# Expert blocks and row gathers on one core: gathers of the U phase bound behind U blocks, columns dealt anew, transposes moved, a score tile widened

## The chip, the cores and the metric

One core of a Trainium2 chip runs the whole program. The metric is the time of one execution on the device in microseconds (us); what counts is the median of several runs. Each run is timed without a profile, and one more execution is profiled. A difference of 0.2% is about what the measurement can tell from no change.

The engines run side by side and wait for each other by semaphores: PE (matrix products), DVE (vector work), ACT (activations and copies), POOL (here: a few vector operations, and the issue of gathers), SP (the issue of plain transfers). Sixteen DMA engines move the data of all queues.

## The reference

One layer of a hybrid decoder: a combined input projection, a convolution branch, a state-space branch, an output projection, and then an expert mixer over 16384 experts. The change touches the mixer alone:

```python
def peer_block(xb, w_q, keys, U, V):
    T = xb.shape[0]
    q = (xb @ w_q).reshape(T, PEER_HEADS, 2, D_KEY // 2)          # 8 heads, 2 halves of 128
    s = jnp.einsum('thcd,hckd->thck', q, keys).astype(jnp.float32) # 128 keys each
    s1, i1 = lax.top_k(s[:, :, 0], PEER_TOPK)                      # 16 of 128
    s2, i2 = lax.top_k(s[:, :, 1], PEER_TOPK)
    cand = (s1[..., :, None] + s2[..., None, :]).reshape(T, PEER_HEADS, PEER_TOPK * PEER_TOPK)
    sc, f = lax.top_k(cand, PEER_TOPK)
    ids = (jnp.take_along_axis(i1, f // PEER_TOPK, axis=-1) * N_KEYS
           + jnp.take_along_axis(i2, f % PEER_TOPK, axis=-1))
    g = jax.nn.softmax(sc, axis=-1)
    act = jax.nn.gelu(jnp.einsum('thkd,td->thk', U[ids], xb).astype(jnp.float32), approximate=False)
    w = (g * act).astype(xb.dtype)
    return jnp.einsum('thk,thkd->td', w, V[ids])
```

Each of the 320 tokens that are left at this point chooses 128 experts (8 heads, 16 each), and its output is the sum of their V rows, weighted by gate times gelu of the U row's product with the token.

## The kernel before, in words

The mixer takes two ways at once. 128 tokens (and 8 more) are **gathered**: for each of their picks, a column of 128 expert numbers is fetched by an indirect transfer that brings 128 rows of 2048 numbers (a U row and a V row side by side, 8 KB) into one of five buffers `wuv`. There are 136 such columns. The other 184 tokens are **dense**: the kernel computes them against all experts, in 128 blocks of U (each 128 experts by 1024, 512 KB) and then 128 blocks of V, and a matrix of gates zeroes what a token did not choose.

The order of the program:

- *Queries and scores* (`for j in range(16)`): 16 blocks of `w_q` give `qT`, and three products with `keys` give the scores of the three token tiles of `KTILES`: 128 gathered tokens, 128 and 64 others. The third product has 64 columns of `qT` as its stationary side. DVE finds the top 16 of the gathered tile at once (`heads`); the other two are left to background tasks (`topk_tasks(1)`, `topk_tasks(2)`).
- *U phase.* `u_block(b)` loads block b into a ring of eight buffers (`eraw`, from SP's queue), and PE makes 8 products, each of which the profile records as two: 16 records to a block. The last product's name goes into `ustep`. Behind each block a `Feed` hands out background tasks, so that all are dealt evenly: up to block 84 (`SB`) the top-k tasks of the dense tokens mixed with `NU[0]` picks; from block 84 on the first half of the gate steps (`g_step`, PE `pg`, DVE `oh`) with `NU[1]` picks.
- *V phase.* `v_block(b)` the same, with the product's name in `vstep`; beside its first 64 blocks the second half of the gate steps and `NU[2]` picks, then the rest of the picks up to block 126.

A *pick* of column n (`pick_row`) is DVE's dot product of the U half with the token (`pick_dot`), two tiny ACT operations, and DVE's weighted sum of the V half of the column before (`pick_sum`), which frees a buffer. Before a dot product, `ahead` issues the gathers of the next columns (four, later two). `gather` issues one on POOL's queue, and ties it to the block that lies `LEAD` = 4 blocks behind the last one issued: it starts only when PE has finished that block. In the kernel before, the list that this counts from leaves out U's first 84 blocks, so that the gathers beside them are tied to no block.

When a dense tile's top 16 are known, `place` transposes the picks and gates on PE into `pix`; `PLACE` names the U blocks behind which the transposes of the two tiles stand in PE's order. PE works in the order of its queue: if such a transpose waits for DVE, all blocks behind it wait.

A scheduler sorts the instructions of each engine by a simulated time, within what these bounds and the data allow.

Of the kernel before, what the change touches and what calls it, by code (L numbers as in the profile page):

```python
# [7 lines left out]
F32 = mybir.dt.float32  # L8
# [15 lines left out]
T = TP + NQ * TS  # L24
# [11 lines left out]
T2 = 320  # L36
# [16 lines left out]
SB = 84  # L53
HB = 64
KTILES = ((0, NGAT), (128, 128), (256, 64))
NU = (42, 28, 37)
LM = (0.05, 0.05, 0.1, 0.5, 0.999)
LOW = 400
NW0 = 3
# [3 lines left out]
DEEP = 4  # L63
NEAR = 2
GLAG = 14
PLACE = (38, 50)
LASTP = 126
XW = 70
XR = 86
# [75 lines left out]
def body(tc, ia, oa, stop=None):  # L145
    nc = tc.nc
    with ExitStack() as top:
# [58 lines left out]
        def pj(name="pj"):  # L206
            return ps.tile([128, PJ], F32, name=name, tag="pj", bufs=3)[:, :T]

        def pj2(name="pj"):
            return pj(name)[:, :T2]  # L210
# [32 lines left out]
        def proj(out, w, act, first=True, last=True):  # L243
            for k in range(KD):
                for c_ in range(2):
                    mm(out, w[0][:, k, :], act(k)[c_], start=(first and k == 0 and c_ == 0), stop=False)
            for k in range(KD):
                mm(out, w[1][:, k, :], act(k)[0], start=False, stop=(last and k == KD - 1))

        def weight(src, i):  # L250
            raw = wp.tile([128, KD, 128], F32, name="wraw", bufs=rb[0])
            nc.sync.dma_start(raw, src[i].rearrange("p (k m) -> p k m", m=128))
            h = wp.tile([128, KD, 128], F32R, name="wh", bufs=2)
            l = wp.tile([128, KD, 128], F32R, name="wl", bufs=2)
            nw[0] += 1
            f_ = lm[0]
            on_dve = int((nw[0] + 1) * f_) > int(nw[0] * f_)
            split(h, l, raw, on_pool=not on_dve, on_dve=lm[0] == 1)
            return h, l
# [3 lines left out]
        def rows(h, l):  # L263
            return lambda k: (h[:, k, :], l[:, k, :])

        def misc(shape, name):
            return ps.tile(shape, F32, name=name, tag="misc", bufs=2)
# [64 lines left out]
        p = misc([128, T], "pn1")  # L332
# [11 lines left out]
        t = tp.tile([128, T], F32, name="rst", tag="yo", bufs=2)  # L344
# [177 lines left out]
        def xbc(g):  # L522
            tiles = [pair(F32, "xg"), None]

            def step(c_, j):
                if c_ == 2:
                    tiles[1] = pair(F32, "bc")
                pf = project(8 * g + c_)
                p = pf[:, :T]
                cat = tp.tile([128, MCAT], F32, name="mcat", bufs=2)  # L530
                cpr, csm = cat_fill(cat, MC, mcache[:, j, :])
                nc.scalar.activation(cpr[:, NM:], p[:, :SQ], AF.Identity, bias=V("b_in", 8 * g + c_))
                nc.scalar.activation(cpr[:, :NM], p[:, T2:], AF.Identity, bias=V("b_in", 8 * g + c_))
                nc.scalar.activation(csm, samp(p[:, SQ:T2]), AF.Identity, bias=V("b_in", 8 * g + c_))
                cat_save(cat, MC, mnew[:, j, :])
                conv_short(cat, j, tiles[c_ // 2][:, c_ % 2, :], pf[:, :MCAT])

            return tiles, [lambda c_=c_, j=j: step(c_, j) for c_, j in enumerate((2 * g, 2 * g + 1, 16 + g, 24 + g))]
# [311 lines left out]
        for g in range(G):  # L850
            new = ssd(g, *tiles, sz)
            if g + 1 < G:
                tiles, steps = xbc(g + 1)
# [48 lines left out]
        for j in range(KD):  # L902
# [4 lines left out]
            p = pj2()  # L907
# [7 lines left out]
        for j in range(KD):  # L915
            w = weight(ia["w_o"], j)
            p = pj2()
# [13 lines left out]
        p = ps.tile([128, T], F32, name="pn2", tag="pb", bufs=1)  # L931
# [30 lines left out]
        qp = qs.enter_context(tc.tile_pool(name="qp", bufs=1))  # L962
# [7 lines left out]
        for c_ in range(2):  # L970
            p = misc([128, 512], "px")
# [4 lines left out]
        p = misc([128, 4], "prs")  # L976
# [7 lines left out]
        def extra_tokens():  # L984
            E0 = NGAT + ND
            nc.gpsimd.memset(acce, 0.0)
            xe = qp.tile([128, 128], F32, name="xe", bufs=2)
            nc.gpsimd.tensor_copy(xe.rearrange("p (q t) -> p q t", t=NX),
                                  rs2[:, None, E0:T2].to_broadcast([128, XQ, NX]))
            p = misc([128, 4], "prs")  # L990
            nc.tensor.matmul(p[:, 3:4], xe, ident[:, 0:1], start=True, stop=True)
            nc.scalar.copy(rsT[:, 3:4], p[:, 3:4])
            for c_ in range(2):
                p = misc([128, 512], "px")
                cs = slice(c_ * 512, c_ * 512 + 512)
                for k in range(4):
                    xe = qp.tile([128, 128], F32, name="xe", bufs=2)
                    nc.gpsimd.tensor_copy(xe.rearrange("p (q t) -> p q t", t=NX),
                                          xT[:, 4 * c_ + k, None, E0:T2].to_broadcast([128, XQ, NX]))
                    nc.tensor.transpose(p[:, k * 128:(k + 1) * 128], xe, ident)  # L1000
                nc.scalar.copy(acce[:NX, cs], p[:NX])
                nc.vector.scalar_tensor_tensor(x2e[:, cs], p, rsT[:, 3:4], n2r[:, cs], op0=OP.mult, op1=OP.mult)

        keys = qp.tile([128, 16, NK], F32, name="keys")
        nc.sync.dma_start(keys, ia["keys"])

        def top16(vals, idx, v, h, late=False):
            L = v.shape[0]
            i_ = nc.vector.max(vals[:L, h, 0:8], v)
            if late:  # L1010
                tc.add_manual_dep(i_.ins, early[0], mybir.DependencyInfo(mybir.DependencyClass.NoSync,
                                                                         mybir.DependencyReason.DATA),
                                  reason="gathered tokens first")
            nc.vector.max_index(idx[:L, h, 0:8], vals[:L, h, 0:8], v)
            nc.vector.match_replace(v, vals[:L, h, 0:8], v, -3.0e38)
            nc.vector.max(vals[:L, h, 8:16], v)
            nc.vector.max_index(idx[:L, h, 8:16], vals[:L, h, 8:16], v)
# [73 lines left out]
        ustep, vstep = [], []  # L1091

        def gather(c):
            u = gp.tile([128, 2 * D], F32, name="wuv", bufs=UV)
            i_ = nc.gpsimd.indirect_dma_start(out=u, out_offset=None, in_=ia["peer_uv"],  # L1095
                                              in_offset=bass.IndirectOffsetOnAxis(ap=gid[:, c:c + 1], axis=0))
            steps = ustep[SB:] + vstep
            if len(steps) > LEAD:
                tc.add_manual_dep(i_.ins, steps[-1 - LEAD], mybir.DependencyInfo(mybir.DependencyClass.Sync,
                                                                          mybir.DependencyReason.DATA),  # L1100
                                  reason="rows after blocks")
            return u

        def ahead(n):
            for i_ in range(n, min(n + (DEEP if len(vstep) <= HB else NEAR), NCOL)):
                if i_ not in pend:
                    pend[i_] = gather(COLS[i_])

        for j in range(16):
            w = weight(ia["w_q"], j)  # L1110
            p = pj()
            proj(p[:, :T2], w, rows(ah[:, :, :T2], al[:, :, :T2]))
            qT = qp.tile([128, T], F32, name="qT", bufs=3)
            nc.scalar.copy(qT[:, :T2], p[:, :T2])
            p = misc([128, 3, NK], "psc")
            for i, (t0, L) in enumerate(KTILES):
                nc.tensor.matmul(p[:L, i], qT[:, t0:t0 + L], keys[:, j, :], start=True, stop=True)
                s_ = sall[:, i - 1, j] if i else kp.tile([128, NK], F32, name="sco", bufs=9)
                nc.scalar.copy(s_[:L], p[:L, i])
                if i == 0:  # L1120
                    top16(sv[i], si[i], s_[:L], j)
            if j == EXTRA:
                extra_tokens()
            if j % (2 * HG) == 2 * HG - 1:
                heads(j // 2 - HG + 1)
            if j == 2 * HG - 1:
                ahead(0)
# [10 lines left out]
        def topk_tasks(i):  # L1138
# [34 lines left out]
            def place():  # L1173
                n_ = min(L, NGAT + ND - t0)
                p = misc([128, 3, 128], "pix")
                for c_, v in enumerate((st[0], st[1], st["g"])):
                    i_ = nc.tensor.transpose(p[:, c_, :L], v[:L], ident[:L, :L])
                    tc.add_manual_dep(i_.ins, ustep[PLACE[i - 1]], mybir.DependencyInfo(mybir.DependencyClass.NoSync,
                                                                              mybir.DependencyReason.DATA),
# [68 lines left out]
        t1, t2 = topk_tasks(1), topk_tasks(2)  # L1248
        bg = mixin(t1[:-1] + t2[:-5] + t1[-1:] + t2[-5:-1], take(NU[0] - 4)) + take(4) + t2[-1:]

# [81 lines left out]
        Sm.append(s1p.tile([128, 128 - SB, ND], F32, name="S1"))  # L1332
        feed = Feed(mixin(g_tasks(0), take(NU[1])), 128 - SB - 2)
        for b in range(SB, 128):
# [65 lines left out]

        feed = Feed(mixin(g_tasks(1), take(NU[2])), HB - 2)
        for b in range(HB):
# [109 lines left out]
```

## Time and profile before

| | |
|---|---|
| median of 3 runs | 1330.94 us |
| lowest, highest | 1330.91, 1332.9 us |
| the profiled execution | 1334.54 us |
| its span, first to last instruction | 1332.8 us |
| PE, DVE, ACT, POOL busy | 1294.1, 993.7, 524.5, 583.1 us |
| moved by the DMA engines | 373.68 MB, of it 142.62 MB by the gathers |

Times in the profile count from the start of the span. A row of a timeline has the start, the duration, the engine, the line and operation, tiles written and read, and in square brackets how long the engine was idle ahead of it and what ended that. A row of busy time by stretches has the stretch, and for each engine its busy time and the number of instructions; then the granted share of PE's clock, the busy share of the DMA engines, and what they moved in GB/s. A group's row has the count, the busy time, the mean in ns, and the idle time of its engine ahead of it. q0 is the queue of the gathers, q1 SP's.

### The profile page before, as it was taken

To read this page: it belongs to the slowest core of one execution; us is meant where nothing else is said; L and a number is where in the kernel's file an instruction comes from. 1 tells how busy PE (TensorE), PEld (TensorE's weight loads), DVE (VectorE), ACT (ScalarE), POOL (GpSimd) and SP (SyncE) were. 2 spreads that over 40 slices of the span, in tenths; PEclk is the share of its full clock that TensorE was granted. 3 is DMA by queue.
4 is the path that set the end of the run, shared out by engine and by line. 5 is a ranking of instruction groups with operands and counts; after the bars stand their busy time and mean duration, and the time that the engine had idled before them with its cause. 6 is when DMAs were issued, how large, how long until landed. Compare 5 with 4: busy or idle time off the path is not lost.

```text
span 1332.8 us, 23897 instructions
## 1 busy us (share of the span) xinstructions
PE 1294.1 (97%) x9004; PEld 1225.6 (92%) x9004; DVE 993.7 (75%) x2324; ACT 524.5 (39%) x1377; POOL 583.1 (44%) x484
## 2 busy tenths in 40 slices
PE   9999999999999999999999898999999999999997
PEld 7888888888888999988999898999999999999997
DVE  7888778877877335799999987458977888644453
ACT  6777777777765444433322221121210111101012
POOL 2477767876684666744222252032332323122210
PEclk9999999999999999999999999999999999999999
DMA  6434453454434344637999999799999999999992
GB/s 242 161 127 170 166 172 129 153 180 150 157 99 159 129 156 143 210 114 277 381 414 415 377 397 414 282 416 413 396 413 414 415 414 416 398 395 415 414 413 107
DMA packets 85892, 373.68 MB, mean 280 GB/s; under 512 B 9984, under 2 KB 15488, under 8 KB 66192
## 3 DMA queue, kind: packets, MB, share of 16 engines
q1 hardware_dynamic: 65024, 227.52, 46.5%
q0 software_dynamic: 19584, 142.62, 26.2%
q10 hardware_dynamic: 1168, 2.02, 0.4%
q8 instruction: 71, 1.16, 0.3%
q14 instruction: 45, 0.37, 0.1%
HBM read 359.05 MB, written 13.06 MB: 279 GB/s over the span
## 4 chain that ended last, share of the span: by engine, by line
PE 73%; DVE 17%; DMA 7%; ACT 2%; issue 1%; POOL 0%; DVEq 0%; ACTq 0%; POOLq 0%
PE pj L159 29%; PE va L1378 21%; PE pj L1284 12%; DMA eraw<-in_uT_dram 3%; DMA eraw<-in_vE_dram 3%; DVE ygat L1215 2%; DVE wuv L1207 2%; PE pst L159 2%; PE pg L1312 1%; PE po L159 1%; PE py L159 1%; DVE pcv L482 1%; PE pdec L159 1%; DVE cand L1060 1%; PE ptr L164 1%
## 5 line engine op out<-in xcount | busy, mean ns | idle before, releaser
L1095 POOL DMA_INDIRECT wuv<-in_peer_uv_dram,gid x136 | 184.2, 1354 | 490.9 <-PE va L1378 151.6
L1284 PE MATMUL pj<-nd,eraw 128*128 128x184 f32 x2048 | 332.6, 323 | 8.7 <-DMA eraw<-in_uT_dram 5.2
L1284 PEld LDWEIGHTS pj<-nd,eraw 128*128 128x128 f32 x2048 | 321.9, 191 | 11.3 <-ACT S L1286 6.9
L227 POOL TENSOR_TENSOR wl<-wraw,wh 128x1024 fp32r<-128x1024 f32 x111 | 267.2, 2408 | 148.2 <-ACT wh L226 77.3
L1378 PE MATMUL va<-S,eraw 128*128 128x184 f32 x2048 | 326.7, 320 | 2.7 <-DMA eraw<-in_vE_dram 2.6
L1378 PEld LDWEIGHTS va<-S,eraw 128*128 128x128 f32 x2048 | 318.8, 190 | 5.9 <-DMA eraw<-in_vE_dram 4.1
L159 PE MATMUL pj<-ah,wh 128*128 128x336 f32 (+1 forms) x768 | 242.5, 327 | 0.7 <-ACT xnf L202 0.7
L159 PE MATMUL pj<-al,wh 128*128 128x336 f32 (+1 forms) x768 | 233.0, 317 | 0.0
L1215 DVE SCALAR_TENSOR_TENSOR ygat<-wuv,scg,ygat 128x1024 f32<-128x1024 f32 x128 | 164.0, 1281 | 52.2 <-ACT scg L1210 50.5
L1207 DVE SCALAR_TENSOR_TENSOR wuv<-wuv,x2m 128x1024 f32<-128x1024 f32 x128 | 156.0, 1219 | 62.8 <-DMA wuv<-in_peer_uv_dram,gid 62.8
L1209 ACT ACTIVATE scg<-scg 128x1 f32<-128x1 f32 x136 | 27.5, 202 | 403.7 <-DVE wuv L1207 403.4
L226 ACT CAST wh<-wraw 128x1024 fp32r<-128x1024 f32 x125 | 131.2, 1050 | 115.2 <-PE pj L159 70.1
L482 DVE SCALAR_TENSOR_TENSOR pcv<-ccat,vec,pcv 128x256 f32<-128x256 f32 x464 | 148.7, 379 | 17.1 <-ACT pcv L480 17.1
L159 PEld LDWEIGHTS pj<-ah,wh 128*128 128x128 f32 x768 | 146.3, 191 | 8.7 <-ACT xnf L202 2.8
L159 PEld LDWEIGHTS pj<-al,wh 128*128 128x128 f32 x768 | 145.8, 191 | 0.7
L159 PE MATMUL pj<-ah,wl 128*128 128x336 f32 (+1 forms) x768 | 136.8, 315 | 1.3 <-DVE wl L227 1.3
L159 PEld LDWEIGHTS pj<-ah,wl 128*128 128x128 f32 x768 | 119.5, 188 | 2.7 <-DVE wl L227 1.6
L1286 ACT ACTIVATE S<-pj 128x184 f32<-128x184 f32 x128 | 38.7, 319 | 140.2 <-PE pj L1284 140.1
L496 DVE SCALAR_TENSOR_TENSOR pj<-mcat,vec,pj 128x360 f32<-128x360 f32 x96 | 56.3, 587 | 3.7 <-ACT pj L494 3.7
L1319 DVE SCALAR_TENSOR_TENSOR S<-pg,S 128x352 f32<-128x352 f32 (+1 forms) x69 | 33.2, 508 | 32.7 <-PE pg L1312 30.4
L202 ACT ACT_TABLE_LOAD x39 | 50.0, 1283 | 0.7
L1210 ACT ACTIVATE scg<-scg,ggw 128x1 f32<-128x1 f32 x136 | 40.0, 294 | 4.3
(365 smaller groups left out, 1645.1 us busy)
## 6 DMA issues: line engine op xcount, KB each, us to landing
eraw<-in_uT_dram SPq DMA_DIRECT2D x128, 512.0 KB
eraw<-in_vE_dram SPq DMA_DIRECT2D x128, 512.0 KB
wraw<-in_w_in_dram SPq DMA_DIRECT2D x80, 512.0 KB
st<-in_state_dram SPq DMA_DIRECT2D x8, 1024.0 KB
out_ssm_s_dram<-st SPq DMA_DIRECT2D x8, 1024.0 KB
wraw<-in_w_mo_dram SPq DMA_DIRECT2D x16, 512.0 KB
wraw<-in_w_q_dram SPq DMA_DIRECT2D x16, 512.0 KB
wraw<-in_w_co_dram SPq DMA_DIRECT2D x8, 512.0 KB
```

The costliest lines, as they stand in the source:

```text
L159: i_ = nc.tensor.matmul(*a_, **kw)
L202: i_ = nc.scalar.activation(out, in_, f, **kw)
L226: (nc.vector.tensor_copy if on_dve else nc.scalar.copy)(h, src)
L227: (nc.gpsimd if on_pool else nc.vector).tensor_tensor(l, src, h.bitcast(F32), op=OP.subtract)
L482: t = nc.vector.scalar_tensor_tensor(o, i_, wv, a_, op0=OP.mult, op1=OP.add)
L496: nc.vector.scalar_tensor_tensor(o, cat[:, w:w + n], wv, o, op0=OP.mult, op1=OP.add)
L1095: i_ = nc.gpsimd.indirect_dma_start(out=u, out_offset=None, in_=ia["peer_uv"], in_offset=bass.IndirectOffsetOnAxis(ap=gid[:, c:c + 1], axi ...
L1207: nc.vector.scalar_tensor_tensor(u[:, :D], u[:, :D], 1.0, x2m if c < NPICK else x2e, op0=OP.mult, op1=OP.mult, accum_out=w)
L1210: nc.scalar.activation(w, w, AF.Copy, scale=ggw[:, c:c + 1])
L1215: nc.vector.scalar_tensor_tensor(a_, u[:, D:], scg[:, c:c + 1], a_, op0=OP.mult, op1=OP.add)
L1284: i_ = nc.tensor.matmul(p[:, :ND], raw[:, k, :], nd[:, k, :], start=(k == 0), stop=(k == KD - 1))
L1378: i_ = nc.tensor.matmul(va[k // 2][:, k % 2], raw[:, k, :], Sv(b), start=False, stop=(b == 127), skip_group_check=True)
```

## The change

Four numbers or places change. The list from which `gather` counts takes in all U blocks. Columns are dealt 46, 26, 36 and 28 to the four stretches instead of 42, 28, 37 and 29. The transposes stand behind U blocks 42 and 55 instead of 38 and 50. The third score product takes 128 columns of `qT`, of which the last 64 are zeros (three fixed tiles of 384 columns, whose ends POOL sets to zero once), and gives 128 rows, of which 64 are used as before.

```diff
-NU = (42, 28, 37)
+NU = (46, 26, 36)
-PLACE = (38, 50)
+PLACE = (42, 55)
 ...
-            steps = ustep[SB:] + vstep
+            steps = ustep + vstep
             if len(steps) > LEAD:
 ...
+        qTs = [qp.tile([128, 384], F32, name=f"qT{i}") for i in range(3)]
+        for t in qTs:
+            nc.gpsimd.memset(t[:, T2:], 0.0)
 ...
-            qT = qp.tile([128, T], F32, name="qT", bufs=3)
+            qT = qTs[j % 3]
 ...
-                nc.tensor.matmul(p[:L, i], qT[:, t0:t0 + L], keys[:, j, :], start=True, stop=True)
+                nc.tensor.matmul(p[:, i], qT[:, t0:t0 + 128], keys[:, j, :], start=True, stop=True)
```

POOL's queue, before: the gathers number 45 to 49 (from 0). `DMASW` is the semaphore of an earlier gather on the same lane, `DVE_49` the release of the buffer, `PE_49` a block.

```order
L1095 DMA wuv<-in_peer_uv_dram,gid 128x2048 [waits DMASW0_49,DVE_49]
L1095 DMA wuv<-in_peer_uv_dram,gid 128x2048 [waits DMASW1_49,DVE_49]
L1095 DMA wuv<-in_peer_uv_dram,gid 128x2048 [waits DMASW2_49,DVE_49,PE_49]
L1095 DMA wuv<-in_peer_uv_dram,gid 128x2048 [waits DMASW3_49,DVE_49,PE_49]
L1095 DMA wuv<-in_peer_uv_dram,gid 128x2048 [waits DMASW4_49,DVE_49,PE_49]
```

And the same lanes now:

```order
L1095 DMA wuv<-in_peer_uv_dram,gid 128x2048 [waits DMASW0_49,DVE_49,PE_49]
L1095 DMA wuv<-in_peer_uv_dram,gid 128x2048 [waits DMASW1_49,DVE_49,PE_49]
L1095 DMA wuv<-in_peer_uv_dram,gid 128x2048 [waits DMASW2_49,DVE_49,PE_49]
L1095 DMA wuv<-in_peer_uv_dram,gid 128x2048 [waits DMASW3_49,DVE_49,PE_49]
L1095 DMA wuv<-in_peer_uv_dram,gid 128x2048 [waits DMASW4_49,DVE_49,PE_49]
```

Numbers 45 and 46 waited for no block and now wait for one; by the semaphores' values, numbers 42 to 50 wait for U blocks 68, 71, 72, 73, 74, 75, 77, 80 and 82, where 47 to 50 waited for 84, 85, 87 and 88.

PE's queue, before: the U blocks around the transposes. A count of 8 is one block.

```order
L1284 MATMUL pj<-nd,eraw 128x184 x264
L1177 MATMUL pix<-cst,pick_8164 128x128
L1177 MATMUL pix<-cst,pick_8225 128x128
L1177 MATMUL pix<-cst,gsm 128x128
L1284 MATMUL pj<-nd,eraw 128x184 x96
L1177 MATMUL pix<-cst,pick_8939 128x64
L1177 MATMUL pix<-cst,pick_8970 128x64
L1177 MATMUL pix<-cst,gsm 128x64
L1284 MATMUL pj<-nd,eraw 128x184 x120
```

And now:

```order
L1287 MATMUL pj<-nd,eraw 128x184 x296
L1180 MATMUL pix<-cst,pick_8178 128x128
L1180 MATMUL pix<-cst,pick_8227 128x128
L1180 MATMUL pix<-cst,gsm 128x128
L1287 MATMUL pj<-nd,eraw 128x184 x104
L1180 MATMUL pix<-cst,pick_8935 128x64
L1180 MATMUL pix<-cst,pick_8984 128x64
L1180 MATMUL pix<-cst,gsm 128x64
L1287 MATMUL pj<-nd,eraw 128x184 x80
```

The first three transposes stand four blocks later and the second three five. On DVE 24 picks stand ahead of the first tile's results instead of 23, and 32 ahead of the second's instead of 29.

PE's queue in the score stage, one piece of the difference: products with `keys` (`psc`) between those of the queries (`pj`).

```order
-L1117 MATMUL psc<-keys,qT 128x128
-L1117 MATMUL psc<-keys,qT 64x128
+L1120 MATMUL psc<-keys,qT_6662 128x128
+L1120 MATMUL psc<-keys,qT_6661 128x128
 L159 MATMUL pj<-ah,wl 128x320 x6
-L1117 MATMUL psc<-keys,qT 64x128
-L1117 MATMUL psc<-keys,qT 128x128
+L1120 MATMUL psc<-keys,qT_6662 128x128
+L1120 MATMUL psc<-keys,qT_6663 128x128
```

All score products are now of one form. Their places are the same but for single swaps.

## Prediction

> **What bounds the kernel now.** I read the page first, then busy time by stretches, then the queues in one stretch, then POOL's timeline and PE's waits.
>
> ```profile
> span 1332.8 us, 23897 instructions
> PE   9999999999999999999999898999999999999997
> DMA  6434453454434344637999999799999999999992
> GB/s 242 161 127 170 166 172 129 153 180 150 157 99 159 129 156 143 210 114 277 381 414 415 377 397 414 282 416 413 396 413 414 415 414 416 398 395 415 414 413 107
> q0 software_dynamic: 19584, 142.62, 26.2%
> eraw<-in_uT_dram SPq DMA_DIRECT2D x128, 512.0 KB
> ```
>
> Each digit is one fortieth of the span, 33.3 us. From the nineteenth on the DMA stands near 415 GB/s, with one clear hole: 282 in slice 26. This is where expert blocks (0.524 MB each, 128 U and 128 V) and the 136 gathers (142.62 MB / 136 = 1.049 MB each) share the engines. The next table cuts that part up; its last two columns are DMA share and GB/s.
>
> ```profile
> core 0: us, PE busy (x) PEld busy (x) DVE busy (x) ACT busy (x) POOL busy (x), PEclk, DMA share, GB/s
> 616.00:640.00 24.00, 21.75 (x123) 19.54 (x121) 23.37 (x109) 7.51 (x25) 9.82 (x10) 0.93 0.98 389
> 640.00:720.00 80.00, 79.08 (x504) 78.17 (x505) 79.69 (x295) 22.00 (x72) 19.88 (x16) 1.00 1.00 400
> 720.00:780.00 60.00, 52.93 (x325) 51.67 (x324) 57.80 (x149) 13.50 (x49) 17.22 (x12) 0.97 0.98 383
> 780.00:803.00 23.00, 23.00 (x150) 23.00 (x149) 17.53 (x24) 6.76 (x27) 12.88 (x8) 1.00 1.02 417
> 803.00:829.00 26.00, 21.51 (x181) 20.28 (x181) 18.79 (x31) 4.25 (x16) 5.24 (x6) 1.00 1.02 414
> 829.00:861.00 32.00, 31.99 (x242) 31.51 (x241) 19.82 (x33) 5.83 (x22) 0.80 (x1) 1.00 0.82 305
> 861.00:870.00 9.00, 9.00 (x60) 9.00 (x59) 0.86 (x2) 1.19 (x4) 2.82 (x3) 1.00 0.84 312
> 870.00:982.00 112.00, 109.83 (x899) 108.13 (x898) 90.08 (x150) 23.09 (x86) 36.72 (x24) 1.00 1.01 409
> 982.00:1144.00 162.00, 160.13 (x1286) 155.83 (x1285) 135.21 (x235) 18.43 (x72) 46.83 (x35) 1.00 1.02 415
> 1144.00:1162.00 18.00, 17.17 (x121) 16.55 (x120) 12.26 (x17) 2.48 (x10) 1.19 (x1) 1.00 1.01 403
> 1162.00:1320.00 158.00, 158.00 (x1016) 158.00 (x1015) 71.97 (x93) 17.10 (x61) 33.08 (x27) 1.00 0.93 372
> ```
>
> The last row is V from block 64 on: 1016 records, 16 to a block, in 158 us: PE without a pause at 2.49 us a block. No transfer can shorten it; a gain must come before 1162. There the DMA is the limit, so I keep a ledger of bytes: what each stretch is short of 415 GB/s, turned into time. 616 to 640: (415-389)*24/415 = 1.5 us; then 2.9, 4.6, 0, 0, **8.5**, 2.2, 1.6, 0, 0.5: 21.8 us in all, half of it between 829 and 870.
>
> ```profile
> 824.42 1.21 POOL L1095 DMA_INDIRECT wuv<-in_peer_uv_dram,gid  x1 [6.64 <-DVE ygat L1215]
> 828.12 1.68 POOL L1095 DMA_INDIRECT wuv<-in_peer_uv_dram,gid  x1 [2.48 <-DVE ygat L1215]
> 861.13 0.94 POOL L1095 DMA_INDIRECT wuv<-in_peer_uv_dram,gid  x1 [31.33 <-PE pj L1284]
> 863.62 0.94 POOL L1095 DMA_INDIRECT wuv<-in_peer_uv_dram,gid  x1 [1.55 <-PE pj L1284]
> 803.00:829.00 26.00, 19.91 (x117) 17.89 (x117) 1.00 1.02 414
> 829.00:861.00 32.00, 31.18 (x194) 29.92 (x193) 1.00 0.82 305
> ```
>
> The hole is a pause of the gathers. Up to number 46 (from 0) they are bound to no block; number 47 is the first that is, to U block 84, and POOL waits 31.33 us for it. The last two rows count U-block records alone: while gathers ran free before the pause, 117 records made 7.3 blocks in 26 us, 3.6 us a block instead of 2.49; in the pause 12.1 blocks came in 32 us and the ring of eight block buffers filled.
>
> ```profile
> DMA packets 1514, 8.30 MB, mean 415 GB/s; under 512 B 162, under 2 KB 162, under 8 KB 840
> q0 software_dynamic: 755, 5.51, 66.6%
> q1 hardware_dynamic: 758, 2.78, 34.7%
> ```
>
> These rows (800 to 820) show why blocks starve: both queues move equally many packets, but a gather's are twice as large, so gathers (q0) take two thirds.
>
> **The change, part by part.** *Binding and columns.* Gathers 47 to 50 no longer wait for blocks 84, 85, 87, 88 but for 75, 77, 80, 82, since four more columns are dealt behind U's first 84 blocks; 42 to 46, free before, wait for 68 to 74. The fifth gather and those before stay free; numbers 5 to 41 get bounds that are no later than the blocks beside which they ran, so these rarely bite. POOL's queue holds only gathers here, so behind a waiting one stands just the next; the one who waits is DVE's dot product. In the pause the DMA had (415-305)*32 us = 3.5 MB free, and 0.9 MB to 870; the four gathers are 4.2 MB. They fit: **-10.7 us** (8.5 + 2.2). Bounds: 0, if the pause turns up elsewhere, and -10.7. I take the full value, because the four bounds lie evenly across the pause and DVE has 12 us free in it (19.82 of 32) for four picks:
>
> ```profile
> L1215 DVE SCALAR_TENSOR_TENSOR ygat<-wuv,scg,ygat 128x1024 f32<-128x1024 f32 x128 | 164.0, 1281 | 52.2 <-ACT scg L1210 50.5
> L1207 DVE SCALAR_TENSOR_TENSOR wuv<-wuv,x2m 128x1024 f32<-128x1024 f32 x128 | 156.0, 1219 | 62.8 <-DMA wuv<-in_peer_uv_dram,gid 62.8
> L1312 PE MATMUL pg<-oh 128*128 128x64 f16 x736 | 30.6, 193 | 0.3 <-DVE oh L1308 0.2
> ```
>
> A pick is 1.22 + 1.28 = 2.5 us, four are 10. Ahead of V block 64 there are now 111 gathers, not 110: 1.049 MB at 415 GB/s is **+2.5 us**; behind it one fewer, which is worth nothing beside PE's 158 us. After U block 84, 60 gathers instead of 63 stand beside 108 blocks: 119.5 MB, 288 us; PE needs 108*2.49 and, for the 38 of 46 steps of the gate matrices that stand behind it, 38/46 of 30.6: 294. So PE is next, and what is late after the hole is gone is PE itself, by little.
>
> A figure of the Trainium skill speaks against this value: DMA: Bandwidth & Descriptors, Specifications, gives about 358 GB/s as the limit of one core's share of HBM. By it the pause would hold only (358-305)*32/358 = 4.7 us, and the sum below would be 3.8 us smaller; the rows sustain 415, so the measurement decides.
>
> *Transposes.* PE waited for DVE ahead of them:
>
> ```profile
> PE pix L1177 <- DVE pick L1061: 5.3, 2, 2.8
> ```
>
> The first set stands four blocks (10.0 us) later, with one more pick (2.5 us) ahead of it on DVE: its wait goes. The second stands five blocks (12.4 us) later with three more picks (7.5 us), but PE comes 2.8 us earlier for the first wait and some 2 us for the next part: 2.8 + 7.5 + 4.8 - 12.4 = 2.7 us of wait stay. The ledger has 4.6 us short from 720 to 780, when PE stalled with a full ring: between -4.6 and +2.7 (the wait comes back and nothing else does) I take half of the gain, **-2.3 us**, one of two waits.
>
> *Third score tile.* Narrow tiles cost PE more than their columns:
>
> ```profile
> 573.47 0.60 PE L1117 MATMUL psc<-keys,qT 128*128 128x128 f32 x4
> 573.83 1.13 PE L159 MATMUL pj<-ah,wl 128*128 128x320 f32 x6
> 591.72 0.75 PE L1117 MATMUL psc<-keys,qT 128*128 128x128 f32 x4
> 592.39 1.16 PE L159 MATMUL pj<-ah,wl 128*128 128x320 f32 x6
> 594.33 0.37 PE pj L159 x3
> 594.73 0.28 DVE sv L1009
> 615.72 8.11 DMA wuv<-in_peer_uv_dram,gid
> ```
>
> Four full-width records hold PE for 0.36 us until the next line starts; the four at 591.72, of which two are the 64-wide ones, for 0.67. So 0.31 us a tile, 16 tiles, at most -5.0. The last three rows are of the chain: PE carries it to 594.7, then DVE to the first gather at 615.72. Seven narrow tiles stand before 594.7: **-2.2 us**; the other nine run beside DVE or the ring. Zero is the other bound. The three memsets cost POOL less than 0.95 us each (a fourfold larger one below) and stand ahead of a wait of 4.09 us: nothing.
>
> ```profile
> 550.72 5.00 POOL L227 TENSOR_TENSOR wl<-wraw,wh 128x1024 fp32r<-128x1024 f32 x2 [4.09 <-PE pj L159]
> 556.67 0.95 POOL L986 MEMSET acce<- 128x1024 f32 x1 [0.94 <-DVE vec L223]
> ```
>
> Sum: -10.7 + 2.5 - 2.3 - 2.2 = **-12.7 us**. The profiled execution took 1334.54 us (span 1332.8), the median is 1330.94; that 0.3% doesn't matter to a difference of microseconds. Forecast: 1318.2 us.
>
> **The rivals.** (1) *Blocks starve in place of the pause.* For it: the equal packet counts. A gather at 5.51 MB / 20 us takes 3.8 us, in which 0.53 MB of blocks land, one block, while PE could use 1.5. If the ring is empty by then, each of the four gathers costs PE 1.3 us: 5.1 us back, 1323.3. Against it: free bytes are free bytes, and gathers 42 to 46 come later. The Trainium skill has it as a rule (DMA: Bandwidth & Descriptors, Queues, rings and completion order: an engine takes turns between queues, packet by packet); by that rule the time is this one, and 755 against 758 packets agree with it. (2) *The pause only moves.* 42 to 46 are held for two to four blocks and the DMA idles at 804 to 829 instead. Then only +2.5 and -2.2 stay: 1331.2. Against it: PE starves there, so blocks take every byte until eight buffers are full. (3) *Everything fills.* All 21.8 us go: 1330.9 - 21.8 + 2.5 - 2.2 = 1309.4. Against it: the shortfalls at 616 to 720 have other causes (a late ACT, DVE at 79.69 of 80). (4) *Slower: the second transposes.* DVE is full until 780, and with both queues full the gather at 824.42 came after 6.64 us of waiting and 1.2 us of the one before, 7.9 us, where a pick takes 2.5. If five picks ahead of the transposes stretch so, DVE is 27 us late, PE stops with a full ring, the gathers bound to its blocks stop too: 1318.2 + 27 = 1345. It decides from some 13 us of lateness on. Against it: DVE was busy for 79.69 of 80 us and 57.80 of 60 up to 780, so landings hardly held it.
>
> **How the numbers follow.** Forecast 0.58, (1) 0.15, (2) 0.10, (3) 0.10, (4) 0.07. This measurement tells 0.2% (2.7 us) from no change: (2) is "same", (4) slower, the rest faster: 0.83, 0.10, 0.07. The range runs from (3) to the point where the hole is half filled and nothing else comes (1330.9 - 5.3 + 2.5 = 1328): 1309 to 1328, which leaves out (2) and (4), 0.17.
>
> **What would show it.** Right: no gap of POOL over 10 us between 800 and 900, that slice of the GB/s row near 415, U block 84 some 8 to 12 us earlier, no wait at the first transposes, score records of one form with 0.11 us between them. V from block 64 still 158 us. Wrong: a new pause of gathers, a wait of PE for the second transposes far over 3 us, or blocks at 3.6 us where the pause was.

## Result, and the profile after

| | before | after |
|---|---|---|
| median, runs beside each other | 1331.3 us (1330.91 to 1332.9, 4 runs) | 1321.76 us (1320.57 to 1323.37, 4 runs) |
| ratio, 95% interval | | 0.9927 [0.991, 0.9944] |
| the profiled execution, its span | 1334.54, 1332.8 us | 1323.37, 1321.6 us |

The change saves 9.5 us by the medians and 11.2 by the two profiled executions. The forecast of 1318.2 was 3.6 us too low; the result lies between it and the first rival's 1323.3, nearer to the rival, and inside the range.

Three lines of the page of after, then its busy time by stretches with the columns of the prediction's table (lines L1284, L1378, L1177, L1312, L1117 of before are L1287, L1381, L1180, L1315, L1120 now):

```profile
span 1321.6 us, 23911 instructions
PE   9999999999999999998999998999999999999997
GB/s 244 162 128 172 161 178 111 174 168 163 156 90 158 130 158 144 200 128 272 354 408 415 378 417 415 414 413 414 415 413 416 414 411 415 387 398 409 413 407 86
```

```profile
616.00:640.00 24.00, 18.66 (x113) 16.39 (x111) 22.46 (x102) 8.63 (x30) 8.69 (x9) 1.00 1.00 406
640.00:720.00 80.00, 79.43 (x499) 79.36 (x499) 79.66 (x289) 21.84 (x72) 19.31 (x15) 0.98 0.99 388
720.00:780.00 60.00, 57.70 (x368) 56.57 (x367) 56.74 (x144) 14.28 (x53) 20.04 (x13) 1.00 1.00 396
780.00:803.00 23.00, 22.58 (x170) 22.32 (x169) 19.50 (x30) 5.33 (x22) 9.07 (x6) 1.00 1.02 414
803.00:829.00 26.00, 22.87 (x170) 21.90 (x169) 18.03 (x32) 4.63 (x18) 5.75 (x5) 1.00 1.02 415
829.00:861.00 32.00, 30.93 (x253) 30.18 (x252) 23.69 (x39) 6.00 (x23) 7.30 (x6) 1.00 1.02 413
861.00:870.00 9.00, 9.00 (x74) 8.83 (x73) 7.52 (x13) 1.47 (x5) 1.88 (x2) 1.00 1.03 416
1151.00:1309.00 158.00, 158.00 (x1016) 158.00 (x1015) 69.33 (x91) 16.61 (x59) 31.05 (x26) 1.00 0.92 365
```

Slice 26 of the GB/s line went from 282 to 414, and 829 to 861 from 305 to 413: the hole is gone. V from block 64 on is the same 1016 records in the same 158 us. Two things are not as good as they look: from 803 to 829 PE is still busy for only 22.87 of 26 us (21.51 before), and 640 to 720 is now short of 415 GB/s by 27*80/415 = 5.2 us, where it was 2.9.

POOL's timeline, all gathers of after that start between 805 and 853, shows how the hole was filled:

```profile
805.67 1.00 POOL L1095 DMA_INDIRECT wuv<-in_peer_uv_dram,gid  x1 [4.75 <-PE pj L1287]
817.01 0.94 POOL L1095 DMA_INDIRECT wuv<-in_peer_uv_dram,gid  x1 [10.33 <-PE pg L1315]
820.21 1.02 POOL L1095 DMA_INDIRECT wuv<-in_peer_uv_dram,gid  x1 [2.26 <-DVE oh L1311]
823.11 0.94 POOL L1095 DMA_INDIRECT wuv<-in_peer_uv_dram,gid  x1 [1.89 <-PE pg L1315]
826.61 1.86 POOL L1095 DMA_INDIRECT wuv<-in_peer_uv_dram,gid  x1 [2.56 <-DVE oh L1311]
830.92 0.94 POOL L1095 DMA_INDIRECT wuv<-in_peer_uv_dram,gid  x1 [2.45 <-PE pj L1287]
839.04 1.19 POOL L1095 DMA_INDIRECT wuv<-in_peer_uv_dram,gid  x1 [7.19 <-DVE ygat L1218]
848.35 1.86 POOL L1095 DMA_INDIRECT wuv<-in_peer_uv_dram,gid  x1 [8.12 <-DVE oh L1311]
852.04 1.19 POOL L1095 DMA_INDIRECT wuv<-in_peer_uv_dram,gid  x1 [1.83 <-DVE ygat L1218]
```

The longest gap is 10.33 us instead of 31.33.

The table below holds all kernels of this study, from their profiled executions. U0, U84 and V64 stand for the first product of that block. MB is what all queues moved from U0 to V64, "short" is that time less the MB at 415 GB/s. The runs' names are explained with the experiments.

| kernel | U0 to U84, us | U84 to V64 | V64 to end | MB | short, us | gathers landed by U84, by V64 |
|---|---|---|---|---|---|---|
| before | 242.9 | 303.2 | 171.4 | 217.34 | 22.4 | 47, 110 |
| b_bind | 232.7 | 302.9 | 171.0 | 217.23 | 12.2 | 46, 110 |
| b_deal | 245.5 | 297.0 | 170.9 | 218.68 | 15.6 | 51, 111 |
| b_place | 240.4 | 301.5 | 170.9 | 217.39 | 18.1 | 47, 110 |
| b_wide | 243.1 | 301.3 | 171.2 | 217.53 | 20.3 | 47, 110 |
| after | 239.1 | 299.2 | 171.0 | 218.79 | 11.1 | 49, 111 |
| a_olddeal | 232.2 | 301.9 | 171.1 | 217.08 | 11.1 | 46, 110 |
| a_free | 242.8 | 299.1 | 171.3 | 218.80 | 14.7 | 51, 111 |
| a_narrow | 237.6 | 300.9 | 171.2 | 218.80 | 11.3 | 49, 111 |
| a_oldplace | 239.5 | 299.7 | 170.9 | 218.75 | 12.1 | 49, 111 |
| c_few_u | 230.4 | 297.6 | 174.3 | 214.56 | 11.0 | 46, 107 |
| c_few_v | 238.3 | 298.4 | 174.3 | 214.69 | 19.4 | 49, 107 |
| d_40 | 227.5 | 299.5 | 175.6 | 214.01 | 11.2 | 44, 107 |
| d_38 | 227.9 | 299.2 | 181.4 | 211.82 | 16.6 | 42, 106 |

Before U0 the change shows in one place: from the first score product to U0 all with narrow tiles take 57.5 us and all with wide ones 54.7 or 54.8. Ahead of that product, where the kernels hardly differ, the traces scatter: it starts between 556.3 and 559.1 us.

A single profiled execution is not exact to a microsecond. That of before is 3.2 us over its median, that of b_place 2.75 under its own (1328.35 and 1331.1).

### The profile page after: what moved, and what is told of

The parts are those of the page before. It is cut to its first block, busy times and chain, and to the rows that moved or that the text cites. A ratio compares the mean times of both kernels' runs of the same rounds, so it can differ in the third digit from the quotient of the medians.

```text
span 1321.6 us, 23911 instructions
## 1 busy us (share of the span) xinstructions
PE 1288.1 (97%) x9004; PEld 1224.5 (93%) x9004; DVE 990.6 (75%) x2324; ACT 522.5 (40%) x1377; POOL 578.9 (44%) x487
## 4 chain that ended last, share of the span: by engine, by line
PE 74%; DVE 16%; DMA 7%; ACT 2%; issue 1%; ACTq 0%; DVEq 0%; SPq 0%
PE pj L159 30%; PE va L1381 22%; PE pj L1287 13%; DMA eraw<-in_uT_dram 3%; DMA eraw<-in_vE_dram 3%; PE pst L159 2%; DVE wuv L1210 2%; DVE ygat L1218 2%; PE pg L1315 1%; PE po L159 1%; PE py L159 1%; DVE pcv L482 1%; PE pdec L159 1%; DMA wuv<-in_peer_uv_dram,gid 1%; DVE si L1017 1%
## 5 line engine op out<-in xcount | busy, mean ns | idle before, releaser
L1095 POOL DMA_INDIRECT wuv<-in_peer_uv_dram,gid x136 | 179.8, 1322 | 487.0 <-PE va L1381 126.1
L1287 PE MATMUL pj<-nd,eraw 128*128 128x184 f32 x2048 | 333.4, 322 | 7.5 <-DMA eraw<-in_uT_dram 3.9
L1287 PEld LDWEIGHTS pj<-nd,eraw 128*128 128x128 f32 x2048 | 320.3, 191 | 9.8 <-ACT S L1289 7.4
L1381 PE MATMUL va<-S,eraw 128*128 128x184 f32 x2048 | 326.1, 320 | 1.8 <-DMA eraw<-in_vE_dram 1.6
L1381 PEld LDWEIGHTS va<-S,eraw 128*128 128x128 f32 x2048 | 318.9, 190 | 3.5 <-DMA eraw<-in_vE_dram 2.2
```

Of the source, the lines that this page charges most:

```text
L1287: i_ = nc.tensor.matmul(p[:, :ND], raw[:, k, :], nd[:, k, :], start=(k == 0), stop=(k == KD - 1))
L1381: i_ = nc.tensor.matmul(va[k // 2][:, k % 2], raw[:, k, :], Sv(b), start=False, stop=(b == 127), skip_group_check=True)
```

## Experiments

**Each part alone in the kernel before.** Four kernels, timed on one chip beside before (1331.81 us).

b_bind, the binding alone:

```diff
-            steps = ustep[SB:] + vstep
+            steps = ustep + vstep
```

> The kernel before with the binding alone: gathers beside U's first 84 blocks are tied to blocks, columns dealt 42, 28, 37 as before. Gathers 36 to 46 now wait for U blocks 62 to 82, number 47 for 84 as before. Theory (bytes: the pause was transfer time thrown away, and the starved blocks ahead of it are its other side): the pause of 31 us is spread out, blocks at 803 to 829 no longer take 3.6 us, U block 84 begins some 8 us earlier, the time is 1323, 8 us less than before (5 to 10). Rival (the pause only moves, since the same 47 gathers stand ahead of block 84): within 2 us of 1331.

Measured: 1324.39 us (1323.92 to 1325.12), ratio 0.9945 [0.9933, 0.9958]: 7.4 us less, close to the theory's 8. Three stretches of its busy time:

```profile
803.00:829.00 26.00, 26.00 (x216) 25.65 (x215) 19.87 (x34) 4.46 (x17) 5.37 (x5) 1.00 1.01 399
829.00:861.00 32.00, 32.00 (x259) 31.65 (x257) 24.84 (x42) 6.31 (x24) 8.10 (x6) 1.00 1.02 413
861.00:870.00 9.00, 9.00 (x80) 8.88 (x79) 7.70 (x13) 1.96 (x8) 1.50 (x2) 1.00 1.02 416
```

Four gathers of POOL's timeline:

```profile
801.93 0.94 POOL L1095 DMA_INDIRECT wuv<-in_peer_uv_dram,gid  x1 [4.46 <-PE pg L1312]
815.82 1.16 POOL L1095 DMA_INDIRECT wuv<-in_peer_uv_dram,gid  x1 [12.96 <-DVE ygat L1215]
818.32 0.94 POOL L1095 DMA_INDIRECT wuv<-in_peer_uv_dram,gid  x1 [1.34 <-PE pj L1284]
821.38 1.16 POOL L1095 DMA_INDIRECT wuv<-in_peer_uv_dram,gid  x1 [2.12 <-PE pj L1284]
```

The queues from 800 to 820 (packets, MB, share of the engines):

```profile
q1 hardware_dynamic: 1704, 5.21, 68.1%
q0 software_dynamic: 356, 2.65, 32.5%
```

The hole is filled here without any gather more ahead of block 84. Number 47 is still bound to block 84; it is the earlier ones that are held back. From the packets of q0, 1.049 MB to a gather, number 41 (from 0) lands at 829.8 instead of 814.4, number 46 at 854.9 instead of 837.6, and 47 at 859.8 instead of 868.4. In the place of the held gathers the blocks come: q1 moves 5.21 MB from 800 to 820 instead of 2.78, PE is busy in all of the 26 us from 803 to 829, and U block 72 starts at 815.4 instead of 825.6.

b_deal, the dealing alone (`NU` 42, 28, 37 to 46, 26, 36):

> The kernel before with the columns dealt 46, 26, 36 alone, gathers beside U's first 84 blocks still tied to no block. Four more gathers run freely ahead of block 84, number 51 is the first that waits. Theory: the pause shrinks from 31 us to some 18, blocks starve at 3.6 us for some 15 us longer, block 84 is no earlier, but 60 instead of 63 gathers stand between it and V block 64: the time is 1326, 5 us less than before (2 to 7). Rival (the dealing does it all, the binding only rarely bites): 1322 or less, as with the whole change.

Measured: 1330.64 us (1328.8 to 1333.58), ratio 0.9988 [0.998, 0.9997]: 1.2 us less, and both expectations missed. Two stretches of its busy time:

```profile
829.00:861.00 32.00, 28.61 (x229) 27.47 (x228) 19.64 (x33) 5.60 (x21) 5.03 (x4) 1.00 1.02 410
861.00:870.00 9.00, 9.00 (x72) 8.94 (x71) 9.00 (x17) 1.97 (x7) 2.59 (x2) 1.00 0.80 274
```

PE's waits for blocks between 803 and 870 (us in total, times, longest), in before:

```profile
PE pj L1284 <- DMA eraw<-in_uT_dram: 4.1, 5, 1.1
```

In b_deal:

```profile
PE pj L1284 <- DMA eraw<-in_uT_dram: 6.2, 8, 1.1
```

And in after; b_bind has no such wait there:

```profile
PE pj L1287 <- DMA eraw<-in_uT_dram: 3.9, 5, 1.1
```

The four gathers fill the hole, 410 GB/s, but they take the bytes of the blocks: PE is busy for 28.61 of 32 us and waits 6.2 us for blocks. U0 to U84 takes 245.5 us, 2.6 more than before, though the DMA moves at full rate. A new short hole follows (274). What comes back is behind U84, where three gathers fewer stand.

b_place, the transposes alone (`PLACE` 38, 50 to 42, 55), and b_wide, the wide tile alone:

```diff
-            qT = qp.tile([128, T], F32, name="qT", bufs=3)
+            qT = qTs[j % 3]
 ...
-                nc.tensor.matmul(p[:L, i], qT[:, t0:t0 + L], keys[:, j, :], start=True, stop=True)
+                nc.tensor.matmul(p[:, i], qT[:, t0:t0 + 128], keys[:, j, :], start=True, stop=True)
```

> The kernel before with the transposes of picks behind U blocks 42 and 55 alone. Theory: PE's two waits of 2.8 us go, and with them half of the 4.6 us that the transfers fell short at 720 to 780: 1329, 2 us less than before (0 to 4.6). Rival: the time is set by bytes later on, and the same bytes wait there: 1331, within 1 us.

> The kernel before with the third score tile 128 columns wide alone. Theory: the first gather starts 2.2 us earlier (seven tiles ahead of it, 0.31 us each), and everything behind follows: 1329, 2 us less than before. Rival: DVE and the ring of block buffers hide it: within 1 us of 1331. A third: all sixteen tiles count, 5 us.

Measured: b_place 1331.1 us (1328.35 to 1333.78), 0.9995 [0.9986, 1.0003], no difference. b_wide 1330.62 us (1328.8 to 1334.49), 0.9992 [0.9982, 1.0001], no difference that can be told, though its U phase starts 2.8 us sooner after the first score product. In both the pause of the gathers is still there, with 292 and 295 GB/s from 829 to 861. In b_place PE no longer waits at the transposes, but from 612 to 862 it waits longer for blocks, and for ACT to take up the U products:

```profile
PE pj L1284 <- DMA eraw<-in_uT_dram: 5.8, 7, 1.2
PE pj L1284 <- ACT S L1286: 4.9, 5, 2.4
```

That is 10.7 us, where before had 4.1 and 2.7.

**Parts undone in the kernel after, and columns moved.** Beside before at 1331.65 us:

a_olddeal (after with `NU` 42, 28, 37):

> The kernel after with columns dealt 42, 28, 37, 29 as before; the binding, the moved transposes and the wide tile stay. After took 1321.8 us, the binding alone 1324.4. By the term of the prediction (the dealing's own effect is one more gather ahead of V block 64, 2.5 us, and the binding fills the pause without it): 1319.3. Rival (the dealing also fills stretches that the binding leaves short, 803 to 829 moved 399 GB/s with the binding alone, and so pays for its gather): 1321.6, no difference from after. Second rival (binding and dealing are needed together): 1324 or more.

Measured: 1319.77 us (1317.35 to 1320.34), 0.9899 [0.9884, 0.9913]. Less than after by 2.0 us, or by 3.7 if the ratios are compared; the intervals just overlap. The traces have 4.2 us: 6.9 less up to U84 and 2.7 more behind it, with the same 11.1 us short. So the dealing, once the gathers are bound, only costs; the prediction's price of one gather was about right, and "fills as much as it costs" and "needed together" fall.

a_free (after without the binding):

> The kernel after without the binding: dealing, transposes and wide tile stay. Theory (without bounds the four more gathers fill the pause at the cost of starving blocks, as with the dealing alone, which took 1330.6; the wide tile starts the U phase 2.8 us earlier): 1327.8. Rival (once the U phase starts earlier a pause of the gathers swallows it, since the end of the pause is set by the same bytes): 1330.

Measured: 1326.92 us (1326.14 to 1328.75), 0.996 [0.9948, 0.9972]. The theory, 0.9 us off: in the U phase the unbound kernel loses 3.7 us against after (242.8 to 239.1).

c_few_u (`NU` 42, 26, 36) and c_few_v (`NU` 46, 26, 32). Both have four gathers fewer than after ahead of V block 64, from two different places:

> The kernel after with columns dealt 42, 26, 36, 32: four picks leave U's first 84 blocks for the stretch behind V block 64. By the ledger of bytes (2.5 us a gather, DMA the limit up to V block 64; U blocks 0 to 83 take 239 us where PE's own work there is 84 blocks of 2.49 and some 5 us of gate steps, 215): four gathers fewer are worth up to 10 us, 1312. Rival (the U phase is held by DVE, whose top-k tasks don't change, or by PE after block 84, whose 294 us leave only 5): 1317. Second rival (V from block 64 on, 158 us of PE, can't take three more gathers): 1322 or more, and that stretch would get longer than 158 us.

> The kernel after with columns dealt 46, 26, 32, 32: four picks leave V's first 64 blocks for the stretch behind them. By the ledger alone 10 us less, 1312. Theory (PE is next there: V blocks 0 to 63 take 177.3 us after the change, and PE's own work is 64 blocks of 2.49 and half the gate steps, 15.3, 174.7 in all): 2.6 us less, 1319.2. Rival (the last stretch gets longer by what the first loses): 1322.

Measured: c_few_u 1315.34 us (1314.78 to 1316.1), 0.9874 [0.9859, 0.9889], the best kernel here, between the ledger's 1312 and the first rival's 1317; c_few_v 1325.5 us (1324.2 to 1327.11), 0.9952 [0.9939, 0.9965], by the ratios 3 us slower than after, give or take 3, and above all that was expected of it. Busy time of after from U0 to U84 and from U84 to V64:

```profile
612.30:851.40 239.10, 226.28 (x1514) 220.98 (x1513) 215.25 (x640) 58.14 (x207) 68.93 (x53) 0.99 1.00 399
851.40:1150.60 299.20, 297.37 (x2367) 291.80 (x2364) 241.51 (x407) 45.76 (x177) 82.37 (x61) 1.00 1.02 413
```

The same of c_few_u:

```profile
611.20:841.60 230.40, 223.16 (x1518) 219.38 (x1517) 205.82 (x626) 56.67 (x202) 59.91 (x50) 1.00 1.00 399
841.60:1139.20 297.60, 297.10 (x2363) 291.61 (x2360) 241.64 (x409) 44.68 (x175) 81.97 (x61) 1.00 1.02 412
```

Of c_few_v from V0 to V64, and from V64 on:

```profile
971.70:1148.10 176.40, 175.39 (x1398) 171.55 (x1397) 134.93 (x235) 18.45 (x72) 35.18 (x32) 1.00 0.99 392
1148.10:1309.00 160.90, 158.81 (x1014) 157.74 (x1013) 79.04 (x101) 18.27 (x66) 31.65 (x29) 1.00 0.95 384
```

And c_few_v's wait of PE for blocks from 1138 on:

```profile
PE va L1381 <- DMA eraw<-in_vE_dram: 2.1, 3, 1.0
```

Four gathers fewer beside U's first 84 blocks (three fewer landed by U84) save 8.7 us: PE has 226.28 us of work in 239.10 there, and the DMA sets the time. Beside V's first 64 blocks they save under 1 us, since PE is busy for 175.39 of 176.40 us; the transfers just fall to 392 GB/s. And in the last stretch, where PE waited for nothing with the 25 gathers of after, 29 are left and PE waits for blocks: V64 to end is 174.3 us instead of 171.0 in both.

**More parts undone, more columns moved.** Beside before at 1332.66 us, on a chip whose runs scatter more (1328.75 to 1337.95), so the ratios count:

> The kernel after with the 64-wide third score product as before. After took 1321.8 us. From the first score product to U block 0 the traces so far show 57.5 us with narrow products and 54.7 with wide ones. Theory (with no pause left to swallow an earlier start of the U phase, the 2.8 us come through whole): 1324.6. Rival (as alone, where the wide tile brought 1.2): 1323.

Measured (after with the narrow tile): 1326.95 us, 0.9957 [0.9939, 0.9975]. Against after's 0.9927 that is 4 us more, give or take 3; the trace has 2.8 us more from the first score product to U0, and U0 to V64 the same (538.5 and 538.3). It fits the theory, but doesn't exclude the rival. PE's timeline in the score stage, in a_narrow:

```profile
590.22 0.75 PE L1117 MATMUL psc<-keys,qT 128*128 128x128 f32 x4
590.89 1.16 PE L159 MATMUL pj<-ah,wl 128*128 128x320 f32 x6
```

The same in after:

```profile
590.35 0.61 PE L1120 MATMUL psc<-keys,qT 128*128 128x128 f32 x4
590.71 1.13 PE L159 MATMUL pj<-ah,wl 128*128 128x320 f32 x6
```

From the start of the four records to the next line: 0.67 us with narrow tiles, 0.36 with wide ones.

> The kernel after with the transposes behind U blocks 38 and 50 as before. The moved transposes alone brought 0.7 us, which is no difference. Theory (the stalls at the transposes let block transfers land, and the ring gives the time back while the DMA is the limit): 1321.8, as after, with waits of PE at the transposes of 5 us and more. Rival (the term of the prediction, half of the 4.6 us that the transfers were short from 720 to 780): 1324.1. Second rival (eight more picks stand in the way on DVE now, and the waits grow well beyond 5 us): 1327 or more.

Measured (after with the transposes at 38 and 50): 1324.68 us, 0.9937 [0.9918, 0.9956], against after's 0.9927 no difference that can be told. PE's wait at the transposes:

```profile
PE pix L1180 <- DVE pick L1061: 6.1, 2, 3.1
```

Two stretches of its busy time:

```profile
720.00:780.00 60.00, 53.94 (x317) 53.18 (x316) 57.27 (x148) 13.42 (x49) 19.28 (x12) 0.91 0.99 386
...
803.00:829.00 26.00, 26.00 (x213) 25.65 (x210) 20.59 (x36) 5.29 (x20) 5.54 (x6) 1.00 1.02 414
```

PE loses 6.1 us at the transposes, and from 803 to 829 it is busy for 26.00 us instead of 22.87: while it stands, blocks come in, and up to 862 it never waits for one (3.9 us in after) and waits 0.6 us for ACT instead of 3.3. U0 to V64 is 539.2 us against 538.3.

> The kernel after with columns dealt 40, 28, 36, 32; 42, 26, 36, 32 took 1315.3. Theory (U blocks 0 to 83 pay 2.0 us a gather: with 42 columns in place of 46 they took 230.4 us in place of 238.3; U blocks 84 to 127 pay nothing for 28 in place of 26, 121.8 us against 121.9): 4 us less, 1311.3. Rival (bytes ahead of V block 64 are what counts, wherever they stand): 1315.3, no difference from 42, 26, 36, 32. Second rival (DVE's top-k tasks or PE hold U's first blocks already): 1315, with gathers' bytes short of 415 GB/s there.

> The kernel after with columns dealt 38, 30, 36, 32. Theory, as for 40, 28, 36, 32 with two more moved: 1307.4, if 30 columns fit beside U blocks 84 to 127, whose 121.8 us are some 2 us over PE's own work there. Rival (that stretch then takes 2.5 us more for each further gather): 1311 to 1315. Second rival (only the bytes ahead of V block 64 count): 1315.3.

Measured: d_40 (`NU` 40, 28, 36) 1317.82 us, 0.9887 [0.9866, 0.9908], no difference from c_few_u, as both its rivals had it; d_38 (38, 30, 36) 1323.22 us, 0.9931 [0.9911, 0.9952], worse, and slower than any of its expectations. The theories of both fell: U0 to U84 shrinks by 2.9 us in d_40 and then no more, since PE is by then busy for 222.89 of 227.5 us and waits for no block, and U84 to V64 takes 1.9 us more. In d_38 the bytes that were not moved early come late: by V64 2.7 MB fewer have moved than in c_few_u, 6.6 us at 415 GB/s, and from V64 on it takes 181.4 us, in which PE waits for blocks:

```profile
PE va L1381 <- DMA eraw<-in_vE_dram: 7.1, 10, 1.0
```

## Why the prediction was right or wrong, step by step

**The hole and its price (-10.7).** That the hole was there, that it would fill to 415 GB/s and that it was the main term were right: the binding alone takes 10.2 us off the time that the transfers were short (22.4 to 12.2) and 7.4 us off the median, and undone in after it costs 5.2 us by the medians and 4.4 by the ratios (a_free). The working also names the right gathers for after: numbers 47 to 50 are the ones that start at 830.92, 839.04, 848.35 and 852.04, inside the former pause, and of those before 42 the bounds hold hardly any (number 41 starts at 799.13, 2.2 us sooner than in before). But it shows where bytes went, not what PE got for them. These rows of after count U-block records alone, as the prediction's last two did:

```profile
803.00:829.00 26.00, 22.23 (x134) 20.51 (x133) 1.00 1.02 415
829.00:861.00 32.00, 29.59 (x180) 27.67 (x179) 1.00 1.02 413
```

And these of b_bind:

```profile
803.00:829.00 26.00, 25.02 (x154) 23.58 (x153) 1.00 1.01 399
829.00:861.00 32.00, 30.95 (x190) 29.46 (x191) 1.00 1.02 413
```

That makes 314 records in after, hardly more than the 311 of before, and 344 in b_bind. In after the bytes that fill the hole are the gathers', and half of the gain from U0 to V64 comes behind U84 (3.8 us ahead of it, 4.0 behind). The binding alone holds 39 to 46 back by 15 to 17 us, so that blocks take the bytes first, and gains 10.2 us ahead of U84 and 0.3 behind. This second way to fill the hole, without a gather more, is what the working missed. The Trainium skill's limit of about 358 GB/s (DMA: Bandwidth & Descriptors, Specifications), weighed there, did not hold with one core at work: the filled stretch moved 413. The prediction's estimate by that figure, 3.8 us, also left out 861 to 870, where by the same estimate the term would be 1.2 us instead of 2.2.

**Columns (+2.5).** The step was one more gather ahead of V block 64, priced as if bytes cost the same wherever they stand. It cost 2.0 us by the medians and 4.2 by the traces (a_olddeal). The net hides two larger moves: three more gathers landed by U84 (6.9 us more, where the DMA sets the time) against two fewer behind it (2.7 us less, where PE is next, as the prediction itself had worked out with 294 us; PE was busy for 297.37 of 299.2). Behind U84 the prediction counted 60 gathers; by the landings there are 62 (63 in before). That the hole fills because four more columns are dealt, as the prediction had it, holds for after but isn't needed: b_bind and a_olddeal fill it without them.

**The first rival, blocks starve.** It came true in part. The dealing alone is that rival: hole full, PE waiting 6.2 us for blocks (4.1 in before). In after PE still waits 3.9 us between 803 and 870, and of the 8.27 MB from 800 to 820 the gathers take 4.45 (5.51 of 8.30 in before); with the binding alone PE doesn't wait at all. The equal turns of the two queues, packet by packet, which the Trainium skill states as a rule (DMA: Bandwidth & Descriptors, Queues, rings and completion order), hold only while both have work: in b_bind, where gathers were held, 1704 packets of blocks went with 356 of gathers.

**Transposes (-2.3).** PE's wait of 5.3 us went entirely, where the prediction kept 2.7 us of it at the second set, and alone that brought nothing that can be told (0.9995: 0.7 us less, 1.9 at most). Undone in after it costs 1.3 us by the ratios, give or take 3.4, and 0.9 by the trace, so that there the 2.3 us are not excluded. The step that failed, in the kernel before at least, is that a stall of PE beside a short stretch of transfers is lost time. The waits change places instead: b_place gains 5.3 us at the transposes and waits 3.9 us more for blocks and ACT, and a_oldplace waits 6.1 us at the transposes and 6.6 us less for blocks and ACT than after.

**Third score tile (-2.2).** The first gather starts 55.8 us after the first score product instead of 57.9, as the seven tiles had it, and the whole score stage is 2.8 us shorter in every trace. Alone it brought nothing that can be told, undone in after 4 us, give or take 3. Why it should count for less while the pause is there is argued, not shown: the pause's end depends on blocks that are limited by the same bytes (from one gather's start to the next the pause is 35.9 us in b_wide, 33.0 in before).

**The sum.** -12.7 became -9.5 by the medians and -11.2 by the two profiled executions. By the table's rows of before and after the 11.2 are 11.3 us less short (hole and transposes, said to be 13.0), 3.5 more for 1.45 MB more ahead of V64 (columns, said to be 2.5), U0 3.0 us earlier (2.8 of it in the score stage; tile, said to be 2.2) and 0.4 behind V64. Part by part it looks worse: the transposes alone bring nothing, the columns cost up to 1.7 more than said, and the hole's 10.7 us are 7.4 in the median for the binding alone. One sentence of the prediction was careless: that the profiled execution's 0.3% "doesn't matter to a difference of microseconds". That execution was 3.2 us over its median, that of after 1.6, and a ledger made against it may count shortfalls that a median run has less of. How much of the 10.7 this explains stays open, since other executions of before have no trace here.

**Signs.** Right: slice 26 at 414, no wait at the first transposes (nor at the second), score records of one form, V's last stretch at 158.00, and no blocks at 3.6 us where the pause was (180 records in 32 us are 2.8). Off: U block 84 came 6.8 us earlier, not 8 to 12, and it was 3.0 already at U0; one gap of POOL was 10.33 us.

## What to carry to other kernels

A hole in the DMA's rate can be closed from either end: pull later transfers forward, or hold earlier ones back so that those on the critical path go first. Here two queues shared the engines and the second was the cheaper one (b_bind's 7.4 us against 1.2 of b_deal); a bound on what is not urgent does it. Price a transfer by the stretch that it stands in: here a gather cost 2 to 3 us beside U's first blocks, next to nothing beside V's first 64 once 36 columns stood there, nothing at first in the last stretch and then 3 us for four; moving four columns from the first to the last (c_few_u) gave 6.4 us more than the change itself.

## What the runs showed of the hardware that was not expected

- From 800 to 820 the DMA engines moved 415 GB/s with two thirds gathers (before) and, by b_bind's rows, (5.21 + 2.65) MB in 20 us, 393 GB/s, with two thirds blocks. From 803 to 829 PE was busy for 21.51 of 26 us in the first and all of them in the second: the mix, not the rate, decided whether PE starved.
- Two records of a 64-column score product behind two of 128 columns cost PE 0.31 us more than two further ones of 128 (0.67 and 0.36 us for the four): a product with half the output rows is the slower one. Not each of the 16 costs that much: the stage is 2.8 us longer, where 16 times 0.31 would be 5.0.
- Executions of one kernel spread over some 5 us (1328.8 to 1333.58 for b_deal), and a profiled one can stand at either end.
